# Moving 128 by 128 transposes from TensorE to VectorE blocks and transfers through HBM, and letting a forced task step alone

## The chip, the cores and the metric

One core of a Trainium2 chip. The metric is the device time of one execution in microseconds (us); the median of several executions is compared. TensorE (PE) does matrix products and, before the change, the transposes; VectorE (DVE), ScalarE (ACT) and GpSimd (POOL) work on tiles; SyncE (SP) only issues transfers, in program order, one behind the other.

## The reference, cut to what matters

A sequence of 256 rows of width 2048 goes through three blocks, all in 32-bit floats:

```python
h = x
for layer in (0, 1):
    u = rms_norm(h, mix_norm_pre[layer])
    # layer 0: stick-breaking attention (8 heads) beside a gated delta rule (8 heads)
    # layer 1: block attention (8 heads) beside dilated attention (8 heads)
    h = h + rms_norm(mixer(u), mix_norm_post[layer])
    u = rms_norm(h, ffn_norm_pre[layer])
    h = h + rms_norm((silu(u @ w_gate) * (u @ w_up)) @ w_down, ffn_norm_post[layer])  # width 5632
# then a third block: pooling beside a state space model, and a gated embedding
```

A head of the mixers is 128 wide. The heads' scores are `q @ k.T`; the product of a feed-forward layer contracts over its 5632 columns. Both need tiles with rows and columns exchanged.

## The kernel before, in words

**Products.** Every weight matrix is read once from HBM in pieces of 256 by 512 (a chunk, 512 KB, tile `wr`), issued by SP in `fetch`. `split` cuts each chunk on ACT and DVE into a rounded high part `wh` and a low part `wl`; the activations are cut in the same way. A unit is one 128-deep slice of a chunk, for both halves `t` of the 256 rows: three products (L329, L330, L331) for each half, six in all. Chunks are loaded some seven chunks ahead (five `wr` buffers) and split three ahead (`SA`; four `wh`/`wl` buffers).

**Order.** `gemm` appends units to one list; `order` puts hooks between them; `run_units` writes the program out unit by unit. After each unit `tick` advances the time `now` by one and lets at most three tasks take their next step. A task is a generator: `yield 4` means that its next step comes four units later, `yield lambda: ...` waits for a condition. All attention heads, the delta rule and the tables of the state space model are such tasks, so their instructions stand between the products. What stands in one engine's queue runs in that order.

**Forced tasks.** `drain(sel)` stands before units that need a task's result. As long as a task of `sel` isn't done, it steps every task there is, those not in `sel` as well, whatever time they had asked for. The first norm (`rms`) is drained before unit 15 of the program. Just ahead of it, at the same unit, a hook spawns `load_gains(1, ...)`, which issues loads of five gain vectors (`gsrc`), asks for 30 units of time, and transposes them on TensorE (L157). The projection of the gates (`ab_proj`) is spawned there too.

**Transposes.** `transposes(src)` (L467) makes four 128 by 128 transposes on TensorE into one PSUM bank. The feed-forward layer has 11 panels of 512 columns in three parts (4, 4 and 3 panels). The evacuation of an up panel makes `mid` (128 by 512) for each half; a task transposes it four or five units later and splits it into `mh` and `ml`, which the down product of that part contracts over. `attn_group` (mixer of layer 1, 4 groups of 4 heads) and `sb` (stick-breaking, 2 groups of 4 heads) transpose queries (`tmq`) and keys (`tmk`) of a group, copy them from PSUM with ACT, and then spawn four head tasks, whose scores are L555 and L556, or L958 and L959. `ssm_prep` transposes eight tables (`bt`, L1218), stores them in HBM as `win` and reads them back in the third block with a POOL transfer (L1378).

**Where the heads' results are needed.** In the mixer of layer 1 the output product's unit 12 is the first that uses the last group's heads; they are drained before its unit 11. In layer 0 the second `sb` group is drained before unit 4 of the output product.

Of the kernel before, what the change touches and what calls it, by code (L numbers as in the profile page):

```python
# [10 lines left out]
F32 = mybir.dt.float32  # L11
# [86 lines left out]
def trunk(ctx: ExitStack, tc: tile.TileContext, I, out):  # L98
# [102 lines left out]
        due.append((now[0] + n, f))  # L201

    def drain(sel):
        while any(not x.done for x in sel):
            for d in due:
                d[1]()
            due.clear()
            moved = [x.step(now[0]) for x in list(tasks)]
            tasks[:] = [x for x in tasks if not x.done]
            assert any(moved)  # L210

    W, nf = {}, [0]
    LA, SA, HEAD, TAIL, EXTRA, CAP = 4, 3, 12, 8, 3, 3
# [245 lines left out]
    def h_src(k):  # L459
        a, b = st["mh"][k // 8]  # L460
        return a[:, k % 8, :], b[:, k % 8, :]

    def transposes(src):

        p4 = aux()
        for i in range(4):
            PE.transpose(p4[:, i * P:(i + 1) * P], src[:, i * P:(i + 1) * P], ident)  # L467
        return p4

    def ffn(layer, gi, begin=None, end=None):  # L470
        phase(begin=begin)
        wg, wu, wd = I["ffn_w_gate"][layer], I["ffn_w_up"][layer], I["ffn_w_down"][layer]
        sg = {}

        def gate_evac(j, t, src):
            s = t2("sg")
            ACT.activation(s, src, AF.Silu, scale=st["rs"][:, t:t + 1])
            sg[t] = s

        def up_evac(p0):  # L480
            def f(j, t, src):
                m = t2("mid")
                DVE.scalar_tensor_tensor(m, src, st["rs"][:, t:t + 1], sg[t], OP.mult, OP.mult)
                mh, ml = st["m"]

                def go():
                    p4 = transposes(m)
                    k = p0 * 4
                    v = p4.rearrange("p (k s) -> p k s", k=4)
                    split_evac(mh[:, k:k + 4, t * P:(t + 1) * P], ml[:, k:k + 4, t * P:(t + 1) * P], v)  # L490
                    yield
                st["mid_tasks"].append(spawn(go(), delay=4 + t))
            return f

        def down_evac(first, last):
            def f(j, t, src):
                acc = cut(st["acc"][t], j)
                if first:
                    ACT.activation(acc, src, AF.Copy)
                    return  # L500
                DVE.tensor_add(acc, src, acc)
                if last:
                    square_sum(acc, st["ssp"], t, j)
                    if j < 3:
                        POOL.tensor_mul(acc, acc, cut(st["wpost"], j))  # L505
                    elif t == 0:
                        post_end(True)
            return f

        for pi, (p0, p1) in enumerate(PARTS):  # L510
            b = len(units)
            for p in range(p0, p1):
                gemm(u_src, wg, KTS, [(p * 512, (p + 1) * 512)], gate_evac, gi=gi)
                gemm(u_src, wu, KTS, [(p * 512, (p + 1) * 512)], up_evac(p - p0), gi=gi)
            units[b]["before"].append(lambda: st.update(m=(big("mh"), big("ml")), mid_tasks=[]))
            c = len(units)
            kts = list(range((p1 - p0) * 4))
            gemm(m_src, wd[p0 * 512:p1 * 512, :], kts, cols(4), down_evac(pi == 0, pi == 2))
            units[c + len(kts) - 6]["before"].append(lambda: drain(st["mid_tasks"]))
            if pi == 0:  # L520
                units[c]["before"].append(post_begin)
            if pi == 2:
                units[c]["before"].append(lambda: load_post(I["ffn_norm_post"][layer]))
            if pi == 2 and end:
                units[c]["before"].append(end)
# [10 lines left out]
    def mix1():  # L536
# [1 line left out]
        done = []  # L538

        def attn_group(g, T):  # L540
            qT, kT = [h4(t4(n)) for n in ("qT", "kT")]
            for n, dst in (("q", qT), ("k", kT)):
                yield lambda: n in T["ready"]
                yield 2
                for t in range(2):
                    p4 = transposes(T[n][:, t, :])
                    ACT.activation(dst[:, :, t * P:(t + 1) * P], h4(p4), AF.Copy)
                    yield 1
            mask = st["masks"][g // 2]
            heads = [spawn(attn_head(g, T, mask, i, qT, kT), gap=2, delay=2 + 3 * i) for i in range(4)]  # L550
            yield lambda: all(x.done for x in heads)

        def attn_head(g, T, mask, i, qT, kT):
            ps = aux()
            PE.matmul(ps[:, :P], qT[:, i, :P], kT[:, i, :P], start=True, stop=True)  # L555
            PE.matmul(ps[:, P:3 * P], qT[:, i, P:], kT[:, i, :], start=True, stop=True)  # L556
            s = t2("s", 3 * P)
            DVE.tensor_add(s, ps[:, :3 * P], mask)
            mx = small("mx", 4, 4)
            rng = (slice(0, P), slice(P, 3 * P))  # L560
            for t in range(2):
                DVE.tensor_reduce(mx[:, t:t + 1], s[:, rng[t]], AX.X, OP.max, negate=True)
            yield 1
            for t in range(2):
                ACT.activation(s[:, rng[t]], s[:, rng[t]], AF.Exp, bias=mx[:, t:t + 1],
                               accum_out=mx[:, 2 + t:3 + t])
            yield 1
            DVE.reciprocal(mx[:, :2], mx[:, 2:4])
            for t in range(2):
                DVE.tensor_scalar(s[:, rng[t]], s[:, rng[t]], mx[:, t:t + 1], None, OP.mult)  # L570
            yield 4
            pt = aux()
            for b in range(3):
                PE.transpose(pt[:, b * P:(b + 1) * P], s[:, b * P:(b + 1) * P], ident)
            ACT.activation(s, pt[:, :3 * P], AF.Copy)
            yield
            if "v" not in T["ready"]:
                yield lambda: "v" in T["ready"]
            mh, ml = st["m"]
            v = T["v"].rearrange("p t (h d) -> p t h d", h=4)  # L580
            po = aux()
            PE.matmul(po[:, :S], v[:, 0, i, :], s[:, :S], start=True, stop=False)  # L582
            PE.matmul(po[:, P:S], v[:, 1, i, :], s[:, S:], start=False, stop=True)
            split_evac(mh[:, 4 * g + i, :], ml[:, 4 * g + i, :], po[:, :S])
# [29 lines left out]
    def mix0():  # L614
# [323 lines left out]
            T["U"] = u  # L938

        def sb(g, T):  # L940
            qT, kT = [h4(t4(n)) for n in ("qT", "kT")]
            for n, dst in (("q", qT), ("k", kT)):
                yield lambda: n in T["ready"]
                yield 2
                for t in range(2):
                    p4 = transposes(T[n][:, t, :])
                    ACT.activation(dst[:, :, t * P:(t + 1) * P], h4(p4), AF.Copy)
                    yield 1
            heads = []
            for i in range(4):  # L950
                T["s"] = False
                heads.append(spawn(sb_head(g, T, i, qT, kT), gap=2, delay=2))
                yield lambda: T["s"]
            yield lambda: all(x.done for x in heads)

        def sb_head(g, T, i, qT, kT):
            ps = aux()
            PE.matmul(ps[:, :S], kT[:, i, :P], qT[:, i, :], start=True, stop=True)  # L958
            PE.matmul(ps[:, S:3 * P], kT[:, i, P:], qT[:, i, P:], start=True, stop=True)  # L959
            zm, e = t2("zm", 3 * P), t2("e", 3 * P)  # L960
            DVE.tensor_add(zm, ps[:, :3 * P], st["sbm"])
            DVE.scalar_tensor_tensor(e, zm, -1.0, zm, OP.mult, OP.min)
# [78 lines left out]
    def ssm_prep():  # L1041
# [155 lines left out]
            yield  # L1197

        for n in ("win", "cp"):
            ssm[n] = drp.tile([P, 64, P], F32, name=n)  # L1200
        ssm["kr"] = drp.tile([64, 32, 256], F32, name="kr")
        ssm["tp"] = drp.tile([8, 16, 64, P], F32, name="tp")
        for e in range(8):
# [7 lines left out]
            DVE.tensor_add(v(o)[:, :, 1:], v(o)[:, :, 1:], v(tm)[:, :, 1:])  # L1211
            ACT.activation(v(o)[:, :, 0], gc(bb)[:, gs, :], AF.Copy)
            yield
            w = t4("wt")
            for j in range(2):
                ps = aux()
                for i in range(4):
                    PE.transpose(ps[:, i * P:(i + 1) * P], o[:, (4 * j + i) * P:(4 * j + i + 1) * P], ident)  # L1218
                ACT.activation(w[:, j * 512:(j + 1) * 512], ps, AF.Copy)
                yield 1  # L1220
            POOL.dma_start(ssm["win"][:, gs, :], w.rearrange("p (g k) -> p g k", g=8))
            yield

        cs_, cx = t4("cs"), t4("cx")
# [63 lines left out]
    def blk2():  # L1288
# [84 lines left out]

        def table(name, e):
            o, src = t4(name), ssm[name]
            if name == "tp":
                src = src.rearrange("r c g k -> (r c) g k")
            POOL.dma_start(o.rearrange("p (g k) -> p g k", g=8), src[:, 8 * e:8 * e + 8, :])  # L1378
# [2 lines left out]
        def ssm_states(ux, q, wi):  # L1381

            g3 = lambda x: x.rearrange("p (g c) -> p g c", c=32)
            for e in range(q, 8, 2):
# [8 lines left out]
                for hh in range(2):  # L1393
                    for j in range(4):
                        g = 2 * j + hh
                        PE.matmul(ps[32 * j:32 * j + 32, hh * P:(hh + 1) * P], ux(e, g), wi[:, g * P:(g + 1) * P],
                                  start=True, stop=True, tile_position=(0, 32 * j))
                wi = None
                vt = t2("vt")
# [231 lines left out]
```

## Time and profile before

| | |
|---|---|
| median of 3 executions | 2844.2 us (2844.18 to 2846.04) |
| the profiled execution | 2845.48 us |
| its span, first to last instruction | 2843.7 us |
| instructions | 36948 |
| mean granted TensorE clock | 0.996 |
| moved by transfers | 552.25 MB |

The span is what the trace shows; 1.78 us of the profiled execution lie around it. Busy times of the engines are sums over the span. A busy PE is a union of pipelined products: the duration that a row gives for one product is longer than the distance to the next one's start, so costs on PE are read from distances between starts.

### The profile page before, as it was taken

How to read it: one execution, taken by the hardware profiler on the slowest of the kernel's cores; microseconds unless marked ns; L12 is line 12 of the kernel's file. 1: busy time of each engine (PE TensorE's matmuls, PEld its weight loads, DVE VectorE, ACT ScalarE, POOL GpSimd, SP SyncE). 2: the span in 40 equal slices, each digit the busy share in tenths (PEclk: the TensorE clock that was granted, in tenths of full speed). 3: DMA queues.
4: the chain of work that ended last, by engine and by line, in shares of the span. 5: the costliest groups of instructions: out<-in, count | busy, mean ns of one | idle time of the engine just before them, and what ended most of it. 6: DMA issues, size and time to landing. Idle time of an engine off the chain costs nothing.

```text
span 2843.7 us, 36948 instructions
## 1 busy us (share of the span) xinstructions
PE 2812.8 (99%) x13599; PEld 2312.8 (81%) x13599; DVE 1771.2 (62%) x2703; ACT 1504.9 (53%) x2380; POOL 192.6 (7%) x290
## 2 busy tenths in 40 slices
PE   7999999999999999999999999999999999999998
PEld 5888888888888778878888888888888887878887
DVE  4777766678666666566666565545555556575555
ACT  4666554655555445555555465545544545555444
POOL 0150410000000011000000000000000001100000
PEclk9999999999999999999999999999999999999999
DMA  6564746576767677755556656666656665875654
GB/s 204 170 183 139 196 151 198 162 209 204 219 212 210 213 212 235 228 172 182 171 170 186 190 179 192 188 193 191 190 191 191 189 207 185 298 249 177 194 192 144
DMA packets 305670, 552.25 MB, mean 194 GB/s; under 512 B 43032, under 2 KB 52816, under 8 KB 305488
## 3 DMA queue, kind: packets, MB, share of 16 engines
q1 hardware_dynamic: 295232, 515.52, 59.8%
q0 software_dynamic: 10224, 34.35, 3.8%
q8 instruction: 107, 1.75, 0.3%
q14 instruction: 75, 0.61, 0.1%
q10 hardware_dynamic: 32, 0.01, 0.0%
HBM read 532.24 MB, written 21.76 MB: 195 GB/s over the span
## 4 chain that ended last, share of the span: by engine, by line
PE 95%; DVE 2%; DMA 1%; ACT 1%; issue 0%; SPq 0%; ACTq 0%; POOLq 0%; POOL 0%; DVEq 0%
PE mm L329 30%; PE mm L331 29%; PE mm L330 29%; PE aux L467 1%; DVE wl L364 1%; PE aux L380 1%; ACT wh L363 0%; PE aux L1359 0%; DMA wr<-in_ev_w_in_dram 0%; DMA wr<-in_ffn_w_up_dram 0%; DMA b<-in_b_im_dram 0%; PE aux L1449 0%; PE aux L1218 0%; PE aux L556 0%; PE aux L582 0%
## 5 line engine op out<-in xcount | busy, mean ns | idle before, releaser
L364 DVE SCALAR_TENSOR_TENSOR wl<-wr,gT,wh 128x512 fp32r<-128x512 f32 x1248 | 884.6, 752 | 545.9 <-ACT wh L363 544.7
L363 ACT ACTIVATE wh<-wr,gT 128x512 fp32r<-128x512 f32 x1248 | 829.8, 716 | 536.8 <-PE mm L331 495.9
L329 PE MATMUL mm<-wh,uh 128*128 128x512 f32 (+1 forms) x2656 | 1058.5, 399 | 2.6 <-ACT uh L360 1.3
L331 PE MATMUL mm<-wh,ul 128*128 128x512 f32 (+1 forms) x2656 | 1032.5, 389 | 1.6 <-DVE ul L361 1.6
L330 PE MATMUL mm<-wl,uh 128*128 128x512 f32 (+1 forms) x2656 | 1030.2, 388 | 1.1 <-DVE wl L242 0.9
L242 DVE TENSOR_TENSOR wl<-wr,wh 128x1024 fp32r<-128x1024 f32 x324 | 401.3, 1243 | 355.6 <-ACT wh L241 355.2
L331 PEld LDWEIGHTS mm<-wh,ul 128*128 128x128 f32 x2656 | 499.6, 188 | 111.0 <-DVE ul L361 6.9
L329 PEld LDWEIGHTS mm<-wh,uh 128*128 128x128 f32 x2656 | 500.4, 188 | 104.8 <-issue 5.7
L330 PEld LDWEIGHTS mm<-wl,uh 128*128 128x128 f32 x2656 | 500.9, 189 | 97.5 <-DVE wl L364 2.1
L241 ACT ACTIVATE wh<-wr 128x1024 fp32r<-128x1024 f32 x324 | 342.5, 1059 | 398.9 <-PE mm L331 389.8
L329 PE MATMUL mm<-wh,mh 128*128 128x512 f32 x832 | 326.7, 393 | 0.0
L331 PE MATMUL mm<-wh,ml 128*128 128x512 f32 x832 | 324.0, 389 | 0.0
L330 PE MATMUL mm<-wl,mh 128*128 128x512 f32 x832 | 323.8, 389 | 0.0
L329 PEld LDWEIGHTS mm<-wh,mh 128*128 128x128 f32 x832 | 156.2, 188 | 32.8 <-issue 1.4
L331 PEld LDWEIGHTS mm<-wh,ml 128*128 128x128 f32 x832 | 156.2, 188 | 32.7
L330 PEld LDWEIGHTS mm<-wl,mh 128*128 128x128 f32 x832 | 156.3, 188 | 31.5
L505 POOL TENSOR_TENSOR acc<-acc,wpost 128x512 f32<-128x512 f32 x12 | 15.3, 1300 | 789.5 <-ACT junk L351 789.5
L360 ACT ACTIVATE uh<-aux 128x512 fp32r<-128x512 f32 x48 | 28.6, 595 | 63.5 <-PE aux L380 63.5
L360 ACT ACTIVATE mh<-aux 128x512 fp32r<-128x512 f32 (+1 forms) x60 | 32.5, 542 | 55.4 <-PE aux L467 39.1
L361 DVE TENSOR_TENSOR ul<-aux,uh 128x512 fp32r<-128x512 f32 x48 | 32.7, 689 | 41.0 <-ACT uh L360 40.8
L361 DVE TENSOR_TENSOR ml<-aux,mh 128x512 fp32r<-128x512 f32 (+1 forms) x60 | 37.1, 619 | 32.9 <-ACT mh L360 32.1
L347 POOL TENSOR_TENSOR rp<-ms,half 128x1 f32<-128x1 f32 x8 | 6.7, 840 | 471.8 <-DVE ms L346 471.8
(445 smaller groups left out, 2033.1 us busy)
## 6 DMA issues: line engine op xcount, KB each, us to landing
wr<-in_ffn_w_gate_dram SPq DMA_DIRECT2D x176, 512.0 KB, 4.4
wr<-in_ffn_w_up_dram SPq DMA_DIRECT2D x176, 512.0 KB, 4.2
wr<-in_ffn_w_down_dram SPq DMA_DIRECT2D x176, 512.0 KB, 4.5
wr<-in_ev_w_in_dram SPq DMA_DIRECT2D x112, 512.0 KB, 3.9
wr<-in_od_w_in_dram SPq DMA_DIRECT2D x96, 512.0 KB, 3.7
wr<-in_w_in_dram SPq DMA_DIRECT2D x64, 512.0 KB, 4.9
wr<-in_ev_w_out_dram SPq DMA_DIRECT2D x32, 512.0 KB, 4.0
wr<-in_od_w_out_dram SPq DMA_DIRECT2D x32, 512.0 KB, 4.5
```

Source lines behind the costliest of these rows:

```text
L241: ACT.activation(hi, r[:, k:k + m, :], AF.Copy)
L242: DVE.tensor_sub(lo, r[:, k:k + m, :], hi.bitcast(F32))
L329: PE.matmul(o, a, wh, start=u["first"], stop=False)
L330: PE.matmul(o, a, wl, start=False, stop=False)
L331: PE.matmul(o, b, wh, start=False, stop=u["last"])
L360: ACT.activation(hi, src, AF.Copy)
L361: DVE.tensor_sub(lo, src, hi.bitcast(F32))
L363: ACT.activation(hi, src, AF.Copy, scale=gain)
L364: DVE.scalar_tensor_tensor(lo, src, gain, hi.bitcast(F32), OP.mult, OP.subtract)
L380: PE.transpose(p4[:, i * P:(i + 1) * P], h[:, t, k * P:(k + 1) * P], ident)
L467: PE.transpose(p4[:, i * P:(i + 1) * P], src[:, i * P:(i + 1) * P], ident)
L505: POOL.tensor_mul(acc, acc, cut(st["wpost"], j))
```

## The change

Four places no longer transpose on TensorE. `turn` transposes on DVE each 32 by 32 block of a 128 by 512 (or 1024) tile, with the blocks put in another order; `away` stores the result in HBM; `back` reads it in four transfers of 32 partitions each, whose pieces are 128 floats long (256 for `win`), which exchanges the blocks. `away` and `back` are issued by SP. The feed-forward task handles both halves of a panel together, and the steps lie 1, 2, 4 and 5 units apart; the first two panels of the down product now run all but the last four slices first (`late`), and the drains stand at other units. In `attn_group` and `sb` one of the two operands is used as it lies in the read tile, in runs of 32, and the other is copied by ACT into the plain order. `sb` is changed as `attn_group` is, with the copy made of the keys. `win` is stored untransposed across blocks, and `back` in `table` replaces the POOL read. `drain` steps the tasks of `sel` alone, and all tasks only when none of `sel` can move.

```diff
     def drain(sel):
         while any(not x.done for x in sel):
-            for d in due:
-                d[1]()
-            due.clear()
-            moved = [x.step(now[0]) for x in list(tasks)]
+            moved = [x.step(now[0]) for x in list(tasks) if x in sel]
+            if not any(moved):
+                for d in due:
+                    d[1]()
+                due.clear()
+                moved = [x.step(now[0]) for x in list(tasks)]
+                assert any(moved)
             tasks[:] = [x for x in tasks if not x.done]
-            assert any(moved)
...
+    def turn(x):
+        n, w = x.shape[1:]
+        y = t4("ty", n * w)
+        for t in range(n):
+            DVE.transpose(y[:, t * w:(t + 1) * w], x[:, t, :].rearrange("p (k b j) -> p b k j", b=4, j=32))
+        return y.rearrange("p (t x) -> p t x", t=n)
+
+    def away(y):
+        d = drp.tile([P, 2, 512], F32, name="td", tag="td", bufs=4)
+        nc.sync.dma_start(d, y)
+        return d
+
+    def back(z, d):
+        n, w = d.shape[1:]
+        for b in range(4):
+            nc.sync.dma_start(z[32 * b:32 * b + 32].rearrange("j (t a) x -> j t a x", t=n),
+                              d.rearrange("(a j) t (b x) -> j t a b x", a=4, b=4)[:, :, :, b])
...
         def up_evac(p0):
             def f(j, t, src):
-                m = t2("mid")
-                DVE.scalar_tensor_tensor(m, src, st["rs"][:, t:t + 1], sg[t], OP.mult, OP.mult)
+                if t == 0:
+                    st["mid"] = t4("mid").rearrange("p (t c) -> p t c", t=2)
+                m = st["mid"]
+                DVE.scalar_tensor_tensor(m[:, t, :], src, st["rs"][:, t:t + 1], sg[t], OP.mult, OP.mult)
+                if t == 0:
+                    return
...
                 def go():
-                    p4 = transposes(m)
+                    y = turn(m)
+                    yield 2
+                    d = away(y)
+                    yield 4
+                    z = t4("tz").rearrange("p (a x) -> p a x", a=8)
+                    back(z, d)
+                    yield 5
...
-                st["mid_tasks"].append(spawn(go(), delay=4 + t))
+                st["mid_tasks"].append(spawn(go(), delay=1))
...
-            gemm(m_src, wd[p0 * 512:p1 * 512, :], kts, cols(4), down_evac(pi == 0, pi == 2))
-            units[c + len(kts) - 6]["before"].append(lambda: drain(st["mid_tasks"]))
+            gemm(m_src, wd[p0 * 512:p1 * 512, :], kts, cols(4), down_evac(pi == 0, pi == 2), late=len(kts) - 4)
+            units[c + 2 * len(kts) - 10]["before"].append(lambda: drain(st["mid_tasks"]))
+            units[c + len(kts) - 6]["before"].append(lambda: drain(st["mid_tasks"][:-1]))
...
         def attn_group(g, T):
-            qT, kT = [h4(t4(n)) for n in ("qT", "kT")]
-            for n, dst in (("q", qT), ("k", kT)):
+            zs = {}
+            for n in "qk":
                 yield lambda: n in T["ready"]
+                y = turn(T[n])
                 yield 2
-                for t in range(2):
-                    p4 = transposes(T[n][:, t, :])
-                    ACT.activation(dst[:, :, t * P:(t + 1) * P], h4(p4), AF.Copy)
-                    yield 1
+                d = away(y)
+                yield 4
+                zs[n] = t4("tz").rearrange("p (a x) -> p a x", a=8)
+                back(zs[n], d)
+            qT, kT = [zs[n].rearrange("p a (k i) -> p k a i", k=4) for n in "qk"]
+            yield 4
+            sT = h4(t4("sT"))
+            for t in range(2):
+                ACT.activation(sT[:, :, t * P:(t + 1) * P].rearrange("p k (a i) -> p k a i", a=4),
+                               qT[:, :, 4 * t:4 * t + 4], AF.Copy)
+                yield 1
...
-            w = t4("wt")
-            for j in range(2):
-                ps = aux()
-                for i in range(4):
-                    PE.transpose(ps[:, i * P:(i + 1) * P], o[:, (4 * j + i) * P:(4 * j + i + 1) * P], ident)
-                ACT.activation(w[:, j * 512:(j + 1) * 512], ps, AF.Copy)
-                yield 1
-            POOL.dma_start(ssm["win"][:, gs, :], w.rearrange("p (g k) -> p g k", g=8))
+            w = turn(o[:, None, :])
+            yield 1
+            POOL.dma_start(ssm["win"][:, e, :], w[:, 0, :])
...
+            if name == "win":
+                back(o.rearrange("p (a x) -> p a x", a=4), src[:, e:e + 1, :])
+                return o.rearrange("p (a g i) -> p g a i", a=4, g=8)
```

## Rows read from the trace of the kernel before

**Rows 1.** The page, part 1: busy us, share of the span, instructions.
```profile
PE 2812.8 (99%) x13599; PEld 2312.8 (81%) x13599; DVE 1771.2 (62%) x2703; ACT 1504.9 (53%) x2380; POOL 192.6 (7%) x290
```
**Rows 2.** Waits of PE: us in total, times, longest us.
```profile
PE aux L157 <- DMA gsrc<-in_norm_gain_dram: 10.6, 1, 10.6
```
**Rows 3.** Timeline of PE around one transposed tile: start us, us, engine, line.
```profile
868.46 0.39 PE L329 MATMUL mm<-wh,uh 128*128 128x512 f32 x1
...
868.91 0.39 PE L331 MATMUL mm<-wh,ul 128*128 128x512 f32 x1
869.15 0.60 PE L467 MATMUL aux<-ident,mid 128*128 128x128 f32 x4
869.50 0.48 PE L329 MATMUL mm<-wh,uh 128*128 128x512 f32 x1
869.82 0.40 PE L330 MATMUL mm<-wl,uh 128*128 128x512 f32 x1
```
**Rows 4.** Groups of PE by line: busy us, mean ns of one.
```profile
L467 PE MATMUL aux<-ident,mid 128*128 128x128 f32 x176 | 26.4, 272 | 0.6 <-DVE mid L483 0.6
...
L1218 PE MATMUL aux<-ident,bt 128*128 128x128 f32 x64 | 9.6, 272 | 0.0
...
L467 PE MATMUL aux<-ident,tmq 128*128 128x128 f32 x48 | 7.2, 272 | 0.0
L467 PE MATMUL aux<-ident,tmk 128*128 128x128 f32 x48 | 7.2, 272 | 0.0
```
**Rows 5.** Timeline of PE around unit 15, the first norm's drain.
```profile
35.18 0.39 PE L331 MATMUL mm<-wh,ul 128*128 128x512 f32 x1
...
46.30 0.77 PE L329 MATMUL mm<-wh,uh 128*128 128x512 f32 x1
...
51.97 0.40 PE L330 MATMUL mm<-wl,uh 128*128 128x512 f32 x1
```
**Rows 6.** Windows behind unit 15: busy us by engine, granted clock (PEclk).
```profile
46.00:48.00 2.00, 1.79 (x5) 1.53 (x6) 0.48 (x2) 0.65 (x2) 0.00 (x0) 0.50 0.90 173
...
52.00:54.00 2.00, 2.00 (x10) 1.66 (x9) 0.00 (x0) 0.67 (x2) 0.00 (x0) 1.00 0.63 159
```
**Rows 7.** Timeline of DVE in the same stretch.
```profile
36.15 1.41 DVE L364 SCALAR_TENSOR_TENSOR wl<-wr,gT,wh 128x512 fp32r<-128x512 f32 x2 [1.18 <-ACT wh L363]
...
41.95 0.17 DVE L402 TENSOR_SCALAR rq<-rs 128x2 f32<-128x2 f32 x1 [2.94 <-POOL rs L400]
```
**Rows 8.** Groups of DVE by line: a block transpose, an evacuation.
```profile
L1369 DVE STREAM_TRANSPOSE gelt<-gel 128x256 f32<-128x256 f32 x8 | 3.5, 438 | 0.0
...
L1017 DVE TENSOR_SCALAR tmq<-mm,rs 128x512 f32<-128x512 f32 x4 | 2.9, 745 | 0.2 <-PE mm L331 0.2
```
**Rows 9.** Transfers: SP's queue; then issues, KB, us to landing.
```profile
q1 hardware_dynamic: 295232, 515.52, 59.8%
...
win<-wt POOLq DMA_DIRECT2D x8, 512.0 KB, 5.6
...
win<-win POOLq DMA_DIRECT2D x8, 512.0 KB, 6.9
```
**Rows 10.** Timeline of PE at both mixers' output products: unit 0, last head's product.
```profile
406.00 0.48 PE L329 MATMUL mm<-wh,ms 128*128 128x512 f32 x1
...
409.73 0.59 PE L987 MATMUL aux<-zm,tmv 128*128 128x256 f32 x2
...
1550.99 0.39 PE L329 MATMUL mm<-wh,mh 128*128 128x512 f32 x1
...
1567.02 0.59 PE L582 MATMUL aux<-s,tmv 128*128 128x256 f32 x2
```
**Rows 11.** Windows in the first feed-forward layer; the last two columns: DMA share, GB/s.
```profile
575.00:580.00 5.00, 5.00 (x24) 4.14 (x23) 0.00 (x0) 0.00 (x0) 0.00 (x0) 1.00 0.86 193
...
600.00:1240.00 640.00, 640.00 (x2986) 523.84 (x2985) 434.98 (x639) 329.45 (x492) 43.89 (x63) 1.00 0.70 215
```
**Rows 12.** Timeline of ACT at the first window's end.
```profile
580.25 5.40 ACT L363 ACTIVATE wh<-wr,gT 128x512 fp32r<-128x512 f32 x8 [7.56 <-DMA wr<-in_ffn_w_up_dram]
```

More of the change, by code (lines that the diff above doesn't have):

```diff
@@ L481, in f @@
             def f(j, t, src):
-                m = t2("mid")
-                DVE.scalar_tensor_tensor(m, src, st["rs"][:, t:t + 1], sg[t], OP.mult, OP.mult)
+                if t == 0:
[4 more added lines that the diff above has]
+                    return
                 mh, ml = st["m"]
                 def go():
-                    p4 = transposes(m)
-                    k = p0 * 4
-                    v = p4.rearrange("p (k s) -> p k s", k=4)
-                    split_evac(mh[:, k:k + 4, t * P:(t + 1) * P], ml[:, k:k + 4, t * P:(t + 1) * P], v)
-                    yield
-                st["mid_tasks"].append(spawn(go(), delay=4 + t))
+                    y = turn(m)
[5 more added lines that the diff above has]
+                    yield 5
+                    k = p0 * 4
+                    for t in range(2):
+                        split_evac(*[x[:, k:k + 4, t * P:(t + 1) * P].rearrange("p k (a i) -> p k a i", a=4)
+                                     for x in (mh, ml)], z[:, 4 * t:4 * t + 4].rearrange("p a (k i) -> p k a i", k=4))
+                        yield 1
+                st["mid_tasks"].append(spawn(go(), delay=1))
             return f
@@ L540, in attn_group @@
         def attn_group(g, T):
-            qT, kT = [h4(t4(n)) for n in ("qT", "kT")]
-            for n, dst in (("q", qT), ("k", kT)):
+            zs = {}
+            for n in "qk":
                 yield lambda: n in T["ready"]
+                y = turn(T[n])
                 yield 2
-                for t in range(2):
-                    p4 = transposes(T[n][:, t, :])
-                    ACT.activation(dst[:, :, t * P:(t + 1) * P], h4(p4), AF.Copy)
-                    yield 1
+                d = away(y)
[5 more added lines that the diff above has]
+            sT = h4(t4("sT"))
+            for t in range(2):
+                ACT.activation(sT[:, :, t * P:(t + 1) * P].rearrange("p k (a i) -> p k a i", a=4),
+                               qT[:, :, 4 * t:4 * t + 4], AF.Copy)
+                yield 1
             mask = st["masks"][g // 2]
-            heads = [spawn(attn_head(g, T, mask, i, qT, kT), gap=2, delay=2 + 3 * i) for i in range(4)]
+            heads = [spawn(attn_head(g, T, mask, i, sT, kT), gap=2, delay=2 + 3 * i) for i in range(4)]
             yield lambda: all(x.done for x in heads)
@@ L554, in attn_head @@
             ps = aux()
-            PE.matmul(ps[:, :P], qT[:, i, :P], kT[:, i, :P], start=True, stop=True)
-            PE.matmul(ps[:, P:3 * P], qT[:, i, P:], kT[:, i, :], start=True, stop=True)
+            v = lambda x: x.rearrange("p (a i) -> p a i", i=32)
+            PE.matmul(v(ps[:, :P]), qT[:, i, :P], kT[:, i, :4], start=True, stop=True)
+            PE.matmul(v(ps[:, P:3 * P]), qT[:, i, P:], kT[:, i], start=True, stop=True)
             s = t2("s", 3 * P)
@@ L940, in sb @@
         def sb(g, T):
-            qT, kT = [h4(t4(n)) for n in ("qT", "kT")]
-            for n, dst in (("q", qT), ("k", kT)):
+            zs = {}
+            for n in "qk":
                 yield lambda: n in T["ready"]
+                y = turn(T[n])
                 yield 2
-                for t in range(2):
-                    p4 = transposes(T[n][:, t, :])
-                    ACT.activation(dst[:, :, t * P:(t + 1) * P], h4(p4), AF.Copy)
-                    yield 1
+                d = away(y)
+                yield 4
+                zs[n] = t4("tz").rearrange("p (a x) -> p a x", a=8)
+                back(zs[n], d)
+            qT, kT = [zs[n].rearrange("p a (k i) -> p k a i", k=4) for n in "qk"]
+            yield 4
+            sT = h4(t4("sT"))
+            for t in range(2):
+                ACT.activation(sT[:, :, t * P:(t + 1) * P].rearrange("p k (a i) -> p k a i", a=4),
+                               kT[:, :, 4 * t:4 * t + 4], AF.Copy)
+                yield 1
             heads = []
@@ L951, in sb @@
                 T["s"] = False
-                heads.append(spawn(sb_head(g, T, i, qT, kT), gap=2, delay=2))
+                heads.append(spawn(sb_head(g, T, i, qT, sT), gap=2, delay=2))
                 yield lambda: T["s"]
@@ L957, in sb_head @@
             ps = aux()
-            PE.matmul(ps[:, :S], kT[:, i, :P], qT[:, i, :], start=True, stop=True)
-            PE.matmul(ps[:, S:3 * P], kT[:, i, P:], qT[:, i, P:], start=True, stop=True)
+            v = lambda x: x.rearrange("p (a i) -> p a i", i=32)
+            PE.matmul(v(ps[:, :S]), kT[:, i, :P], qT[:, i], start=True, stop=True)
+            PE.matmul(v(ps[:, S:3 * P]), kT[:, i, P:], qT[:, i, 4:], start=True, stop=True)
             zm, e = t2("zm", 3 * P), t2("e", 3 * P)
@@ L1199, in ssm_prep @@
         for n in ("win", "cp"):
-            ssm[n] = drp.tile([P, 64, P], F32, name=n)
+            ssm[n] = drp.tile([P, 8, 1024] if n == "win" else [P, 64, P], F32, name=n)
         ssm["kr"] = drp.tile([64, 32, 256], F32, name="kr")
@@ L1213, in ssm_prep @@
             yield
-            w = t4("wt")
-            for j in range(2):
-                ps = aux()
-                for i in range(4):
-                    PE.transpose(ps[:, i * P:(i + 1) * P], o[:, (4 * j + i) * P:(4 * j + i + 1) * P], ident)
-                ACT.activation(w[:, j * 512:(j + 1) * 512], ps, AF.Copy)
-                yield 1
-            POOL.dma_start(ssm["win"][:, gs, :], w.rearrange("p (g k) -> p g k", g=8))
+            w = turn(o[:, None, :])
+            yield 1
+            POOL.dma_start(ssm["win"][:, e, :], w[:, 0, :])
             yield
@@ L1395, in ssm_states @@
                         g = 2 * j + hh
-                        PE.matmul(ps[32 * j:32 * j + 32, hh * P:(hh + 1) * P], ux(e, g), wi[:, g * P:(g + 1) * P],
+                        PE.matmul(ps[32 * j:32 * j + 32, hh * P:(hh + 1) * P].rearrange("p (a i) -> p a i", a=4), ux(e, g), wi[:, g],
                                   start=True, stop=True, tile_position=(0, 32 * j))
```

## The prediction

> **What bounds the kernel now.** I read four views. First the page's busy shares: PE is busy for 2812.8 of 2843.7 us, DVE for 62% and ACT for 53% [rows 1]. A busy PE alone proves little, since products overlap, so the second view is the timeline of PE: products start 0.225 us apart (868.46 to 868.91 is two steps), without gaps [rows 3]. PE issues as fast as it can, and what is taken out of its queue shortens the run, if nothing else becomes late. The third view is PE's waits: one is long, 10.6 us in one piece, on a gain vector's transfer [rows 2]. The fourth is the windows, to see how much room DVE and the transfers have where the new work falls: in the first feed-forward layer DVE is busy for 435 of 640 us and the transfer engines for 70% [rows 11].
>
> **Transposes leave PE.** The rows to count are `mid` 176, `bt` 64, `tmq` 48, `tmk` 48 [rows 4]: 336 transposes, 84 groups of four. A group's price is read from starts: from the last product before it (868.91) to the second one after it (869.82) are 0.91 us, where two plain steps are 0.45 [rows 3]. So 0.46 us a group, and 84 x 0.46 = 38.6 us. The upper bound is the busy column of the four rows, 26.4 + 9.6 + 7.2 + 7.2 = 50.4 us [rows 4], which counts overlap with neighbours; the lower one is 0.43 a group (36), as a start can be read to 0.01 us and both ends of the two distances enter. I take 38.6, because the distance is what PE's queue loses.
>
> **The first norm's drain.** Before unit 15 the old `drain` steps every task, so also the one that loads the gains: it issues its loads and, one round later, its transpose, thirty units before its time. PE stands behind that transpose until the load has landed. The last product before it starts at 35.18, the next at 46.30 [rows 5]: 11.1 us, less a step, is 10.9 lost. Then the granted clock is 0.50, which is 1.2 GHz of 2.4, until the window at 52 shows 1.00 again [rows 6]: thirteen products from 46.30 to 51.97 take 5.67 us instead of 2.95 [rows 3, 5], 2.7 more. Together 13.6 us. With the new `drain` the norm's task can always move, so it is stepped alone, and the gains keep their 30 units.
>
> What is late next? DVE waits there for the norm's result until 41.95 [rows 7], and this wait stays. Behind it stand two evacuations of 0.745 [rows 8] and the next low part: 41.95 + 0.17 + 1.49, then half of a 1.41 us pair [rows 7], is 44.3. PE meanwhile has unit 15 and three chunks that are already split (the pair at 36.15 is the third [rows 7]): 35.4 + 7 units of 1.36 (six steps) is 44.9, and the low part is wanted one product later. It is covered by well under a microsecond, so I take 1 us off, with bounds 0 and 10 (if another load, that of the gates' weights, holds DVE as the gains held PE). Gain 12.6. The Trainium skill (TensorE: Matmul & The Clock Gate, Why this matters for your kernels) advises against idle gaps between bursts of products because the clock falls; the rows agree, with 0.50 behind an idle stretch of about 11 us [rows 6], and by both the 2.7 us come back with the gap.
>
> **What DVE, ACT and PE get instead.** A block transpose of 128 by 256 took 438 ns [rows 8]; at twice that at most for 512 columns, a panel adds 1.75 us to DVE, 22 panels and the 24 tiles of queries and keys 60 us, the eight tables 14 us: 74 on 1771 over the run, at 68% in the fullest long window [rows 11]. Hidden behind PE; without cover, 74. ACT loses more copies than it gets. No row shows a 32-bit product whose moving operand comes in runs of 32, as the scores and the `win` products now read it. The bounds are 0 and 0.66 us for each of 24 heads (a pair of score products doubled, since heads' pairs are about 0.6 long in the timeline, nearest row L582 at 0.59 [rows 10]), 16 us. I take 0: such a product spends about four times the time per column of the main products, so its reads have slack.
>
> **The round trip.** 34 times (22 panels, 12 query and key tiles) SP issues one store and four loads that did not exist. Landing: a store of 512 KB into HBM took 5.6 us, a read 6.9 [rows 9]. From `turn` to the split are 2 + 4 + 5 steps, 15 us, against 1.8 + 5.6 + 6.9 and the issue of four transfers; from the split to the first use are 12 more units in the parts of four panels, 4 in the part of three. Load: a packet of SP's queue costs 0.598 x 16 x 2843.7 / 295232 = 0.092 us of one engine [rows 9]. The read has 32 x 8 x 4 = 1024 pieces, so 5.9 us of all sixteen at most, the store 1.5: 7.4 us in each panel's 65 us (32 units of its own and 16 of the down product, at six steps of 0.225 [rows 3]). That lifts 70% to 81%. The dearer question is order: SP works in sequence, so a store that waits for `turn`, or a read that waits for the store's landing, holds the weights queued behind. The trace has such a hold: ACT stood 7.56 us without weights [rows 12] and DVE and ACT did nothing from 575 to 580, while PE was busy for all of these 5 us [rows 11]. So a hold of under 8 us is free. The store follows `turn` by 2.7 us and the read follows the store by 5.4, so I expect holds of 1 to 3 us. Cost 0, upper bound 20 (the one stretch at 560 to 600, where the tables' loads have used this slack already, and some panels).
>
> The Trainium skill (VectorE: DVE Perf Modes, Rules for kernel authors) speaks against the change: a 128 by 128 transpose belongs on TensorE if PSUM will do as its target. Here the row says 0.46 us a group on the engine that bounds the run [rows 3]; by the rule the 38.6 us would stay, and the sum would be 2837.
>
> **Forced heads.** In `attn_group` the keys used to reach the heads after 2 + 1 + 1 + 2 steps; now after 2 + 4 + 4 + 1 + 1 + 2: eight steps later. In the mixer of layer 1 the last head's product came at 1567.02, behind unit 8 of the output product that began at 1550.99; eight later is unit 16, and the drain is before unit 11. In layer 0 the last head's product came at 409.73, behind unit 1 from 406.00 [rows 10]; eight later is unit 9, the drain is before unit 4. Both are forced now: two or three rounds written out back to back, in which PE waits for ACT and DVE. At some 1 us a round I take 5 us together. Bounds: 0, and 5 units of 1.36 at each place with nothing won back, 14.
>
> **The sum.** Against the profiled execution, 2845.5: 2845.5 - 38.6 - 12.6 + 5 = 2799.3. It lies 1.3 above the median of the runs shown, so for the median 2844.2 - 46.2 = **2798 us**.
>
> **The rivals.**
> 1. *The first norm gives little back.* DVE, or PE at the gates' product, waits for the next load in SP's queue. For: the cover is under 1 us [rows 7]. Against: in the new order weights are issued before the gains. With 10 of 13.6 lost: 2807.
> 2. *The forced heads cost their whole delay,* and the strided operands something: 9 to 20 us more, 2812.
> 3. *PE won more than the distance shows,* up to the busy column, and the heads are free: 2844.2 - 50.4 - 13.6 = 2780.
> 4. *SP's queue starves the weights* (the other side). Place: each of the 34 round trips, at the read behind the store. Price: nothing up to a hold of 8 us, then each further microsecond 34 us; it cancels the whole gain from 9.4 us on. For: the store alone takes 5.6 us to land. Against: 5.4 us of steps lie between. At 10 us: 2798 + 68 = 2866.
> 5. *The transposing reads are slow in the transfer engines.* At the 30% free in 65 us [rows 11], some 20 us of a round trip are hidden. At four times the price above, 30 us, each panel would lose 10: 2798 + 220 = 3018. The Trainium skill (VectorE: DVE Perf Modes, The three transpose paths) warns of such a case, a transpose by a plain copy's strides, 19 times slower when the innermost stride at the target is large. Here the pieces are whole runs of 128 floats, and no row shows them slow.
>
> **Chances.** My forecast 0.62; rival 1 0.12; rival 2 0.11; rival 3 0.07; rival 4 0.06; rival 5 0.02. A measurement of this kernel can tell about 0.2% (5.7 us) from no change. Faster: the forecast and rivals 1 to 3, 0.92; same, rival 4 at a hold near 9.4 us, 0.02; slower, the rest of it and rival 5, 0.06. The range leaves out rivals 4 and 5 and the outer part of 2 and 3: low with half of the excess of 50.4 over 38.6 and of rival 3's other gains, 2789; high from rival 2 plus part of the queue's upper bound, 2816.
>
> **What would show it.** Right: no L157 wait near 46, clock 1.00 there; `mid` gone from PE's rows; PE's main products still 0.225 apart in the panels; short PE waits on ACT or DVE around unit 11 of the output product in layer 1 and unit 4 in layer 0. Wrong: PE waits for `wl` or `wh` once per panel, with ACT behind them waiting for `wr`; SP's time before `away` or `back` above 8 us; or a new long wait in the first 60 us.

## The result and the profile after

The changed kernel takes 2800.03 us (median of 4, 2799.45 to 2800.52) against 2844.38: a ratio of 0.9844, 95% interval 0.9829 to 0.9858. The forecast was 2798. The medians lie 44.4 us apart. The span of the profiled executions fell from 2843.7 to 2797.7, by 46.0 us; the sum of the terms was 46.2. That two of the terms were off in opposite directions, so that the closeness is in part luck, is told below.

The page after, part 1 and the packets of SP's queue in part 3, answer to [rows 1] and to the first row of [rows 9]:

```profile
PE 2770.6 (99%) x13263; PEld 2277.7 (81%) x13263; DVE 1813.4 (65%) x2779; ACT 1487.6 (53%) x2352; POOL 187.1 (7%) x282
...
q1 hardware_dynamic: 341728, 555.38, 65.5%
```

PE has 336 instructions less and 42.2 us less busy time, and is still busy for 99% of a span that is 46.0 shorter: it was the bound and is the bound. DVE has 42 us more, SP's queue 46,500 packets and 40 MB more. None of that shows in the time by itself.

PE's waits after, the longest first (us in total, times, longest), answer to [rows 2]:

```profile
PE aux L1283 <- DMA cs<-in_c_im_dram: 3.8, 1, 3.8
PE aux L157 <- DMA ident<-in_cst_dram: 3.0, 1, 3.0
PE mm L334 <- DVE ul L364: 1.6, 5, 0.4
PE aux L618 <- DVE s L614: 1.5, 1, 1.5
...
PE aux L844 <- ACT cv L798: 1.1, 1, 1.1
```

The 10.6 us on the gains are gone. Three waits of over 1 us are new: 3.8 us on a load of the state space model's output tables, which the forecast did not name; 1.5 us on a head's weights `s`, one of the forced heads that it did name; and 1.1 us on `cv`, a tile of the delta rule.

The windows after (busy us of PE, PEld, DVE, ACT, POOL; granted clock; DMA share; GB/s) answer to [rows 6] and [rows 11]:

```profile
40.00:60.00 20.00, 20.00 (x113) 16.34 (x112) 10.89 (x18) 8.26 (x14) 1.67 (x3) 1.00 0.82 273
...
550.00:600.00 50.00, 50.00 (x222) 41.10 (x221) 37.97 (x98) 27.91 (x45) 0.00 (x0) 1.00 0.91 231
600.00:1220.00 620.00, 616.19 (x2814) 503.52 (x2813) 447.62 (x641) 315.57 (x467) 44.11 (x63) 1.00 0.76 235
```

From 40 to 60 PE is busy throughout at 2.4 GHz. In the stretch from 550 to 600, where I had put part of the queue's upper bound, transfers run at 0.91 and PE loses nothing. The 3.8 us are lost in the third window.

### The profile page after: what moved, and what is told of

It is laid out like the page before. It is cut to its first block, busy times and chain, and to the rows that moved or that the text cites. A ratio compares the mean times of both kernels' runs of the same rounds, so it can differ in the third digit from the quotient of the medians.

```text
span 2797.7 us, 36621 instructions
## 1 busy us (share of the span) xinstructions
PE 2770.6 (99%) x13263; PEld 2277.7 (81%) x13263; DVE 1813.4 (65%) x2779; ACT 1487.6 (53%) x2352; POOL 187.1 (7%) x282
## 4 chain that ended last, share of the span: by engine, by line
PE 95%; DVE 3%; ACT 1%; issue 1%; DMA 1%; SPq 0%; ACTq 0%; POOLq 0%; POOL 0%; DVEq 0%
PE mm L332 30%; PE mm L334 30%; PE mm L333 30%; DVE wl L367 1%; PE aux L383 1%; PE aux L1407 0%; DMA wr<-in_ev_w_in_dram 0%; PE aux L490 0%; PE aux L1500 0%; DMA cs<-in_c_im_dram 0%; PE aux L626 0%; DVE ul L364 0%; PE aux L600 0%; ACT wh L366 0%; PE aux L1322 0%
## 5 line engine op out<-in xcount | busy, mean ns | idle before, releaser
L332 PE MATMUL mm<-wh,uh 128*128 128x512 f32 (+1 forms) x2656 | 1050.7, 396 | 2.5 <-ACT wh L366 1.3
L332 PEld LDWEIGHTS mm<-wh,uh 128*128 128x128 f32 x2656 | 499.5, 188 | 106.6 <-issue 5.7
L332 PE MATMUL mm<-wh,mh 128*128 128x512 f32 x832 | 325.6, 391 | 0.0
L332 PEld LDWEIGHTS mm<-wh,mh 128*128 128x128 f32 x832 | 156.2, 188 | 33.4 <-issue 1.4
L354 ACT ACTIVATE junk<-h 128x512 bf16<-128x512 f32 (+1 forms) x50 | 30.5, 610 | 14.6 <-DVE h L1598 13.8
L500 ACT ACTIVATE sg<-mm,rs 128x512 f32<-128x512 f32 x44 | 29.9, 690 | 14.4 <-PE mm L334 14.4
```

Source lines behind the costliest of these rows:

```text
L332: PE.matmul(o, a, wh, start=u["first"], stop=False)
L354: ACT.activation(junk[:, :src.shape[-1]], src, AF.Square, accum_out=ss[:, t, j:j + 1])
```

## The experiments

Each kernel was timed beside the kernel before on the same chip; times are medians. Differences are against 2800.0, or, for experiments 1 and 2, against the kernel before that ran beside them. A line of code has another number in each kernel (L329 before is L332 in the changed kernel); the tiles keep their names.

**1. The kernel before with the new drain only.**

```diff
-            moved = [x.step(now[0]) for x in list(tasks)]
+            moved = [x.step(now[0]) for x in list(tasks) if x in sel]
+            if not any(moved): ...
```

> The kernel before with only the new drain: all transposes stay on TensorE. If the prediction's second term is right (the gains' transpose, forced thirty units early, stops PE for 10.9 us and halves its clock for 2.7 us more), this is 13 to 14 us faster than before: 2831. If the wait only moves to the next load in SP's queue, the gain is under 4 us: 2841 or more. If drains at other places gain as well, it is under 2827.

Measured 2834.34 against 2844.82, ratio 0.9962 (0.9948 to 0.9976): 10.5 us; its profiled span is 12.3 shorter. At the stall itself all of the forecast comes back: the same product starts 13.8 earlier, as these rows show, first of the kernel before, then of this one:

```profile
51.57 0.56 PE L329 MATMUL mm<-wh,uh 128*128 128x512 f32 x1
```
```profile
37.74 0.39 PE L331 MATMUL mm<-wh,uh 128*128 128x512 f32 x1
```

One to three microseconds go again in the following mixer. A wait for `gl` of 1.1 us in all is the largest piece that its profile names; that the delta rule's pieces now meet other neighbours in the queues is my reading, which no run isolates.

**2. The kernel before, old drain, gains spawned one unit later.**

```diff
-                         HEAD + 3: [lambda: spawn(load_gains(1, len(gains)))]}
+                         HEAD + 3: [], HEAD + 4: [lambda: spawn(load_gains(1, len(gains)))]}
```

> The kernel before with the old drain; only the task that loads the gains is spawned one unit later, behind the first norm's drain instead of ahead of it. The gates' projection is still forced there. If the gains' load alone makes the stall, this gives the same as the new drain, 2831. If the gates' projection, forced in the same drain, holds the products too (its weights' load lands about as late), half or less of it comes back: 2838 to 2844.

Measured 2839.13, ratio 0.9979 (0.997 to 0.9989): 5.7 us, half of what the new drain gives. The wait list of PE of this kernel, and its windows behind the drain:

```profile
PE aux L668 <- ACT abs L360: 5.1, 1, 5.1
```
```profile
44.00:46.00 2.00, 0.00 (x0) 0.00 (x0) 0.42 (x1) 0.39 (x2) 0.00 (x0) 0.73 1.09 377
46.00:48.00 2.00, 1.92 (x9) 1.11 (x10) 1.94 (x4) 2.00 (x5) 0.00 (x0) 0.50 0.95 239
```

With the gains out of the way PE stands for 5.1 us before the gates' projection (L668), which the same drain also forced, and the clock halves again. So the stall had two causes, one behind the other, and what repaired it is that the drain leaves alone what it was not asked for; moving one task does half.

**3. The changed kernel with the old drain** (experiment 1's edit the other way).

> The changed kernel with the old drain. Sum of the prediction without its second term: 2800 + 13.6 = 2814, if the two parts of the change add up. If stepping all tasks at the heads' drains costs or saves something in the new order (the last heads are late now, and the old drain drags the delta rule along), it lies more than 2 us away from that: by the forecast of 5 us for forced heads, at most 2819.

Measured 2813.42: 13.4 us slower than with the new one. PE's waits show the old stall in its place, and the wait on the output tables beside it:

```profile
PE aux L157 <- DMA gsrc<-in_norm_gain_dram: 10.5, 1, 10.5
PE aux L1281 <- DMA cs<-in_c_im_dram: 3.7, 1, 3.7
```

At the forced heads the old drain neither helps nor hurts: `s` waits 1.5 us in both. But the 13.4 are not the drain's alone. Behind its 3.7 us on the output tables this kernel's granted clock fell to 0.50, and main products started 0.43 apart until 873.9; behind the same wait the changed kernel kept 1.00 (the last section has the rows). By the starts of the same products in both traces that is 2.6 us of the 15.1 between the two profiled spans. It leaves 12.5 for the drain, close to the 12.3 of experiment 1's span.

**4. Feed-forward products transposed on TensorE again.**

```diff
-                    y = turn(m)
...
+                    p4 = transposes(m)
...
-            gemm(m_src, wd[p0 * 512:p1 * 512, :], kts, cols(4), down_evac(pi == 0, pi == 2), late=len(kts) - 4)
+            gemm(m_src, wd[p0 * 512:p1 * 512, :], kts, cols(4), down_evac(pi == 0, pi == 2))
```

> The changed kernel with the feed-forward products transposed on TensorE again, as before (also their drain and the order of the down product). By the distance between starts, 0.46 us a group, 44 groups: 20 us slower, 2820. By the busy column, 26 us: 2826. If the 22 round trips through SP's queue had cost something that they give back here (single waits for weights or for a load behind them), less than 20: 2812 to 2818.

Measured 2817.14: 17.1 slower. The 3.8 us wait is absent from this kernel's list. With it, 17.1 + 3.8 = 20.9 for 44 groups, 0.47 each: the distance between starts was the right price, the busy column (26) was not.

**5. Queries and keys transposed on TensorE again** (both `attn_group` and `sb` as before, drains as changed).

> The changed kernel with queries and keys transposed on TensorE again (24 groups of four). By distance between starts: 24 x 0.46 = 11 us slower, 2811, if the heads that are forced by the new delay cost nothing. The prediction gave them 5 us: then only 6 us slower, 2806. If they cost their whole delay, it would not be slower at all: 2800 or less.

Measured 2810.53 (2806.93 to 2811.55): 10.5 slower by medians; the spans of the two profiled executions lie 7.5 apart. Its PE still waits on the output tables, but for 1.2 us less than the changed kernel's, and not for `s` or `cv`:

```profile
PE aux L1265 <- DMA cs<-in_c_im_dram: 2.6, 1, 2.6
```

With the 1.2 booked, 11.7 by medians and 8.7 by spans stand against 11 for 24 groups, so the later heads cost between nothing and 2.3 us, not 5.

**6. Input tables transposed on TensorE again, read by POOL.**

> The changed kernel with the state space model's input tables transposed on TensorE again and read back by POOL. 16 groups: 16 x 0.46 = 7.4 us slower, 2807. The tables' task takes eight units longer so, which moves its later loads away from the panel's read ahead of them in SP's queue: if the 3.8 us wait on those loads hangs on this coincidence, it goes, and the time is 2803 to 2804.

Measured 2804.55: 4.5 slower, not 7.4, and the 3.8 us wait is absent here too. 4.5 + 3.8 = 8.3 for 16 groups, of which 0.9 is a wait on `cpo` that is new in this kernel. Two different removals take the wait away, one by removing the panel's read, the other by moving the tables' loads away from it.

**7. The wait on the output tables.** The timeline of SP in the changed kernel (start, us, engine, line), and PE's instruction that waits:

```profile
845.02 3.11 SPq L483 DMA_DIRECT2D tz<-td  x4
848.18 0.60 SPq L1275 DMA_DIRECT2D cs<-in_c_re_dram  x1
848.82 2.00 SPq L1275 DMA_DIRECT2D cs<-in_c_im_dram  x1
```
```profile
855.96 0.63 PE L1283 MATMUL aux<-ident,cs 128*128 128x128 f32 x4 [3.81 <-DMA cs<-in_c_im_dram]
```

The four reads of a panel stand in SP's queue directly ahead of these loads and occupy it for 3.11 us; PE reaches the transposes at 852.15, 3.3 us behind the issue of the second load, and waits until 856. In the kernel before, the same load was issued 7.5 us ahead of them:

```profile
883.96 0.64 SPq L1227 DMA_DIRECT2D cs<-in_c_im_dram  x1
```
```profile
891.43 0.60 PE L1235 MATMUL aux<-ident,cs 128*128 128x128 f32 x4
```

The task gave the loads four units of time. The edit gives nine:

```diff
                                   I[x[i]][0].rearrange("(b g) c n -> (g c) b n", g=8))
-        yield
+        yield 9
```

> The changed kernel with five more units of time between the loads of the state space model's output tables and their transposes on PE. In the changed kernel PE waits 3.8 us there, once, because a panel's read stands before these loads in SP's queue. If the wait is lateness of that one load, it goes: 2796. If the following steps then wait in its place, or the shift makes another forced task late, it stays 2800.

Measured 2795.52 (2795.39 to 2795.6), 4.5 less than the changed kernel; ratio to the kernel before 0.9827 (0.9812 to 0.9842). The wait is gone from PE's list. It was the lateness of that load.

**8. How long SP may be held.** Three kernels put store and read of a feed-forward panel back to back, once, twice and four times with the same data. The edit of the second; the first has no added lines, the third has the two added lines three times:

```diff
                     d = away(y)
-                    yield 4
                     z = t4("tz").rearrange("p (a x) -> p a x", a=8)
                     back(z, d)
+                    d = away(y)
+                    back(z, d)
```

> The changed kernel, where a feed-forward task issues the read directly behind the store, so that SP stands for the store's landing (3.7 us median) with the weights queued behind it, 22 times. If a hold of under 8 us is free, as the prediction says, the time stays 2800 within 2 us. If SP has no such slack, about 4 us for each panel: 2880.

> As the kernel with store and read back to back, but the round trip is made twice for each panel with the same data. SP is away from the weights for about 14 us (a landing of 4, four issues of 2.4 together, a landing of 5.7, four issues). With a slack of 8 us: 6 us for each panel, 2930. With the chunks that are already split counted as well (loads some 7 us ahead of need, splits another 6 to 8 ahead of PE), it is about covered: 2800 to 2820.

> The round trip four times for each panel, back to back: SP is away for about 30 us. With a slack of 8 us: 22 us for each of 22 panels, 3280. With a slack of 13 to 14 us: 16 us each, 3150. If the weights that share the transfer engines with it matter too, more.

Measured 2804.55, 2888.82 and 3181.27. SP's timeline at the same panel, with one trip and then with two:

```profile
671.76 0.34 SPq L476 DMA_DIRECT2D td<-ty  x1
677.53 2.54 SPq L483 DMA_DIRECT2D tz<-td  x4
680.16 2.08 SPq L228 DMA_DIRECT2D wr<-in_ffn_w_down_dram  x4
```
```profile
691.12 0.34 SPq L476 DMA_DIRECT2D td<-ty  x1
...
699.09 0.60 SPq L476 DMA_DIRECT2D td<-ty  x1
...
705.11 14.05 SPq L228 DMA_DIRECT2D wr<-in_ffn_w_down_dram  x9
```

And PE behind the second of these:

```profile
709.85 0.79 PE L332 MATMUL mm<-wh,mh 128*128 128x512 f32 x1 [5.24 <-ACT wh L244]
...
712.71 0.63 PE L334 MATMUL mm<-wh,ml 128*128 128x512 f32 x1
713.13 0.63 PE L332 MATMUL mm<-wh,mh 128*128 128x512 f32 x1
```

At this panel the weights stand for 8.4 us with one trip (671.76 to 680.16) and for 14.0 with two; then PE waits 5.24 us and runs at a step of 0.42, half the clock. With one trip all panels together cost 4.5 us, with two 88.8, and two more trips add 292, or 6.6 a trip and panel, where the second trip holds SP for 6.0 here (699.09 to 705.11).

These sums are not spread evenly over the 22 panels. Windows over the first and the second feed-forward layer, of the changed kernel and then of the one with two trips (behind the length stands PE's busy time with its count of products):

```profile
535.00:1255.00 720.00, 715.24 (x3258) 583.19 (x3257) 520.49 (x796) 373.82 (x569) 47.12 (x66) 1.00 0.76 230
1650.00:2300.00 650.00, 650.00 (x2870) 538.21 (x2869) 369.49 (x475) 327.40 (x454) 2.96 (x3) 1.00 0.72 212
```
```profile
535.00:1335.00 800.00, 738.98 (x3249) 595.64 (x3249) 517.83 (x794) 371.07 (x568) 47.21 (x66) 0.96 0.72 221
1735.00:2400.00 665.00, 654.85 (x2863) 537.33 (x2862) 365.82 (x474) 323.65 (x455) 4.68 (x4) 1.00 0.70 225
```

Two trips make nearly the same products take 80 us more in the first layer and 15 in the second. PE is idle for 61 and 10 us, and the mean granted clock is 0.96 and 1.00. Of the 61 us, 9.7 are the wait on the output tables' load and 4.8 one on another small load (`psrc`). With one trip, all that PE loses in the profiled execution, 5.7 us, arises in the first layer. A panel of the second layer, SP and then PE:

```profile
1739.55 0.34 SPq L476 DMA_DIRECT2D td<-ty  x1
...
1751.67 7.83 SPq L228 DMA_DIRECT2D wr<-in_ffn_w_up_dram  x6
```
```profile
1757.17 0.50 PE L333 MATMUL mm<-wl,uh 128*128 128x512 f32 x1 [0.35 <-DVE wl L367]
```

Here a hold of 12.1 us costs PE a wait of 0.35, while 14.0 in the first layer cost 5.24 and half the clock behind it, and 8.4 with one trip a wait of 1.5. Hold less wait, the slack is 7 to 11 us at the panels of the first layer where PE waits for weights alone, and some 12 in the second; why it differs stays open. Beyond it each further microsecond is paid, and more where the clock falls. My alternative, that the chunks already split extend the slack to 13 or 14, is refuted by the second kernel.

**9. A faster version.** On top of experiment 7's edit the heads of the second mixer start closer together:

```diff
-            heads = [spawn(attn_head(g, T, mask, i, sT, kT), gap=2, delay=2 + 3 * i) for i in range(4)]
+            heads = [spawn(attn_head(g, T, mask, i, sT, kT), gap=2, delay=1 + 2 * i) for i in range(4)]
```

> The changed kernel with the later transposes of the output tables (2795.5 alone) and with the heads of the second mixer started 1 + 2 i units after their group instead of 2 + 3 i, so that the last one comes four units earlier and less of it is forced. By the wait of 1.46 us that the changed kernel's PE shows at that drain: 2794. If four heads closer together wait on each other's pieces on DVE and ACT, no gain or a loss: 2795 to 2798.

Measured 2794.36 (2793.51 to 2795.01), ratio to the kernel before 0.9822 (0.9807 to 0.9836); the 1.5 us wait for `s` is gone from PE's list. The 1.2 us against experiment 7's 2795.52, which was not timed beside it, are no more than the runs scatter; the 4.5 of experiment 7 are clear of it.

## Why the prediction was right, step by step

**Transposes leave PE, 38.6.** Right in mechanism and size: 0.47 a group where it stands alone (experiment 4). Reading the price off the distance between starts, and not off the busy column, decided between 2798 and 2786. One sum beside it was wrong: the 2837 for transposes left on TensorE kept the 5 us of the forced heads, which no longer arise then. Without them it is 2832, and experiment 1, which is that kernel, took 2834.34.

**The first norm's drain, 12.6.** Right: 13.4 by medians on the changed kernel, 2.6 of the profiled execution's the clock at another place (experiment 3), and 10.5 on the kernel before. The step that DVE's wait for the norm stays and is covered held. These rows of PE around unit 15, which answer to [rows 5], have the starts a plain step apart, and DVE begins its next low parts, eight in 5.38 us, at 43.20, where the prediction had the first one ready at 44.3:

```profile
35.02 0.39 PE L334 MATMUL mm<-wh,ul 128*128 128x512 f32 x1
35.25 0.39 PE L332 MATMUL mm<-wh,uh 128*128 128x512 f32 x1
```
```profile
43.20 5.38 DVE L367 SCALAR_TENSOR_TENSOR wl<-wr,gT,wh 128x512 fp32r<-128x512 f32 x8
```

What I had as a rival, the gates' weights holding PE in place of the gains, is real (experiment 2), but only where they are forced as well. I had weighed it as a matter of SP's order; it was a matter of who else the drain steps.

**DVE and the strided operands, 0.** Right in size. The block transposes took 684 ns where 876 were allowed (and 1235 where 1752 were), and the score products of `attn_group` with runs of 32 take 272 and 380 ns, those of the kernel before the same. The reason given for 0 was not right: two products of 256 columns take 0.43 us from start to start (L582 at 1567.02 [rows 10], L583 at 1567.45), about twice the 0.225 of a main product of 512, and not four times. Why runs of 32 cost nothing stays open. Groups of PE and of DVE by line, the latter for [rows 8]:

```profile
L600 PE MATMUL aux<-tz,sT 128*128 128x256 f32 x32 | 9.6, 380 | 0.0
...
L599 PE MATMUL aux<-tz,sT 128*128 128x128 f32 x32 | 6.1, 272 | 0.0
```
```profile
L471 DVE STREAM_TRANSPOSE ty<-mid 128x512 f32<-128x512 f32 x44 | 28.4, 684 | 0.0
...
L471 DVE STREAM_TRANSPOSE ty<-bt 128x1024 f32<-128x1024 f32 x8 | 9.9, 1235 | 0.0
```

**The round trip, 0 with an upper bound of 20.** For the weights right: the store lands after 3.7 us and the four reads after 5.7 each, in the median:

```profile
td<-ty SPq DMA_DIRECT2D x34, 512.0 KB, 3.7
tz<-td SPq DMA_DIRECT2D x136, 128.0 KB, 5.7
```

Between them lie four steps, 5.4 us, so SP isn't held. The slack that I read as 8 us was measured as 7 to 11 in the first layer and some 12 in the second. The reading itself was wrong: the 7.56 us [rows 12] are ACT's idle time, while SP's weights stood there for 13 us, between these two rows of the kernel before (the first ends at 559.26), and PE lost nothing:

```profile
549.79 9.47 SPq L225 DMA_DIRECT2D wr<-in_ffn_w_up_dram  x4
...
572.53 5.45 SPq L225 DMA_DIRECT2D wr<-in_ffn_w_up_dram  x4
```

Rival 4 is shown as a mechanism by experiment 8, with the holds from which it decides, and shown not to act. Rival 5 is refuted: the four reads landed after 5.7 us, where it needed a round trip of over 20. The rule of the Trainium skill cited there (VectorE: DVE Perf Modes, The three transpose paths) compares a strided copy with the hardware's own transposing copy, which no run here makes; on these runs of 128 floats the reads were not slow enough to be seen in the time. But the term was mis-sized at zero: I asked only what the 34 trips do to the weights, and not to the other loads in SP's queue. The tables' loads had just enough time before; behind a panel's read they are 3.8 us late.

**Forced heads, 5.** The place was right. The timeline of PE in the second mixer shows two heads' transposes back to back, the second waiting for DVE:

```profile
1531.50 0.49 PE L618 MATMUL aux<-ident,s 128*128 128x128 f32 x3
1533.45 0.61 PE L618 MATMUL aux<-ident,s 128*128 128x128 f32 x3 [1.46 <-DVE s L614]
```

The size was too large: 1.5 us of waiting here, 0.3 at the same place of the first mixer, nothing to 2.3 in all by experiment 5. That a round costs little because most of the forced head's chain is already under way in the other engines is my guess; no run shows it. So 5 was put down for at most some 2 and 0 for 3.8, and the two errors nearly cancel: that the total came within 2 us is in part luck.

**What stays open.** The four removals (17.1, 10.5, 4.5, 13.4) add up to 45.5, near the whole 44.4. But two of them each take the wait of 3.8 us along and a third takes 1.2 of it; with it booked once the parts give 50.5, and some 48 without the 2.6 us of clock in experiment 3. The three or four microseconds between are not assigned; the executions of experiment 5 alone scatter over 4.6.

## What to carry to other kernels

When one engine is busy for 99% and issues at its plain step, price what leaves its queue by the distance between starts before and after it; then look for lateness elsewhere. A hand-written order that forces work early can stop the whole machine on a load that nobody needs yet: let a forced wait advance only what it waits for. And when transfers are added to an in-order queue, list every load that stands behind them, small and rare ones too, with the time that each had to spare. Read that time from the issuing queue itself, and separately in each layer.

## What the hardware showed that I had not expected

An idle PE does not always lose its clock, and the length of the wait alone does not tell. Four of these kernels wait for the same load of the output tables, each behind main products at a plain step. Behind 3.81 us (the changed kernel) the granted clock stays at 1.00, 2.4 GHz:

```profile
852.00:854.00 2.00, 0.15 (x1) 0.00 (x0) 0.00 (x0) 1.76 (x3) 0.00 (x0) 1.00 1.27 193
854.00:856.00 2.00, 0.04 (x1) 0.07 (x2) 0.00 (x0) 0.72 (x2) 0.00 (x0) 1.00 1.16 224
856.00:858.00 2.00, 2.00 (x12) 1.70 (x13) 1.38 (x3) 0.00 (x0) 0.00 (x0) 1.00 0.99 248
```

Behind a shorter wait, 3.66 us (experiment 3), it was 0.50, 1.2 GHz:

```profile
868.29 1.09 PE L1281 MATMUL aux<-ident,cs 128*128 128x128 f32 x4 [3.66 <-DMA cs<-in_c_im_dram]
```
```profile
870.00:872.00 2.00, 2.00 (x7) 1.48 (x6) 2.00 (x4) 0.00 (x0) 0.00 (x0) 0.50 1.04 381
```

It fell behind 3.01 us too (experiment 8, one trip):

```profile
858.53 1.09 PE L1282 MATMUL aux<-ident,cs 128*128 128x128 f32 x4 [3.01 <-DMA cs<-in_c_im_dram]
```
```profile
858.00:860.00 2.00, 1.47 (x6) 1.41 (x7) 0.35 (x1) 0.00 (x0) 0.00 (x0) 0.54 1.32 230
```

Behind 2.60 us (experiment 5) main products again start 0.23 apart. So of these waits the longest kept the clock and two shorter ones lost it. What decides, these runs do not show. The Trainium skill (TensorE: Matmul & The Clock Gate, Why this matters for your kernels) warns of idle gaps between bursts of products; two of these waits agree with it, and the one of 3.81 us cost only itself.
